# DMA landing times given to a kernel's own instruction planner, and a solve whose blocks are staged elsewhere: hybrid DeltaNet and windowed attention layer on Trainium2

## The chip, the cores and the metric

The kernel runs on one core of one Trainium2 chip. The metric is the device time of one execution in microseconds (us). Three runs of the kernel before gave 1277.84, 1278.94 and 1281.57 us; the median is 1278.94 us. Within the core, PE does matmuls and transposes, DVE, ACT and POOL are the three engines for elementwise work, and SP issues all DMA transfers of this kernel on one in-order queue. Each engine runs its instructions in the order in which they were written to it, and waits on semaphores for what it needs.

## The reference

The reference is one encoder layer on a sequence of 2048 rows of 1024. Cut to what matters here:

```python
h = rms_norm(x, norm_w)
proj = h @ w_in                      # one projection, split into ten parts
dn = fwd + bwd                       # gated DeltaNet, 4 heads of 128, both directions
sw = windowed_gqa_with_sinks(...)    # 8 query heads, window of 128
mix = concat([rms_norm(dn) * silu(dn_z), sw * silu(sw_z)])
x = x + mix @ w_out

# the DeltaNet, for each head, direction and chunk:
m     = strict_lower((k * beta) @ k.T * decay)
t_inv = inverse(eye + m)             # unit lower triangular
u, w  = t_inv @ (v * beta), t_inv @ (k * beta * exp(g))
# then a scan over the chunks with a 128x128 state:
v_new = u_i - w_i @ state
o     = (q_i * exp(g_i)) @ state + a_i @ v_new
state = state * exp(g_last) + k_dec.T @ v_new
```

The kernel works in chunks of 128 rows, so there are 16 chunks for each head and direction, and 32 triangular 128x128 matrices to be inverted for each head.

## The kernel before

**Stages.** `phase_a` normalises x, makes the projections (each product in three float32r matmuls from high and low parts, L191 to L193 and L202 to L204), the convolution, and the windowed attention. Results go to DRAM: `kq_d` and `v_d` hold keys, queries and values of the DeltaNet, `zdn_d` its gates, `mix_sw` the attention output. `phase_b` holds the DeltaNet and the output projection. Its four heads run through these steps:

- `pre_front(h)` loads keys and queries (`kq`, a ring of two buffers, L654), values (`vt`, L656) and decay rows (`dc`, L664, broadcast over the partitions), transposes them on PE, makes the Gram products `gh` on PE, scales them into `ma` on DVE (L703), and writes the triangular matrices to DRAM as `m_d` (L708).
- `solve(h)` reads back only the 32x32 diagonal blocks of the 32 matrices, four per matrix, one block to a partition. The forward direction's blocks land in the upper half of the tile `X` (L731), the other direction's in the lower half of `L` (L732). DVE copies the first, transposed, into `L` (L734). POOL then sets `X` to zero (L735) and its diagonal to one (L736), and 31 pairs of DVE instructions do the elimination (L741, L745). `X` goes to DRAM as `x_d` (L746).
- `invert(h)` brings the inverses of the blocks back, one matrix row to a partition (`xc`, L757), transposes them on DVE (`xt`, L758), and places them on the diagonals of three 128x128 work matrices `e1`, `e2`, `e3` (L763, L765, L767; all three are buffers named `iv` in the trace). Each takes four POOL copies of 32 partitions. Five batches of products `pi` (L772) then assemble the inverse in place in `ma`. This is done four times for each head, `hi` = 0 to 3.
- `scan(h)` is the serial chain over the 16 chunks, both directions interleaved: it loads `kqc` (L810), and each step goes through `pk`, `r`, `py`, `yk`, `po` and the new state `S` (L812 to L837). `post` normalises the output, applies the gate `zt` and writes `mix_dn` (L882).

The program issues scan(h), pre_front(h+1), solve(h+1), invert(h+1) for h = 0 to 2, then scan(3). Beside them, 32 units of the output projection for the attention half ("fill", products `pcs`, L599 to L601) can run at any time; each loads `mxs`, `xrs` and in the later half `zcs` into small rings. At the end `out_dn` reads `mix_dn` back as `mxd` and does the DeltaNet half (`pcd`, L561 to L563).

**The order of the work** does not follow the program text. `set_order` takes all instructions, builds their dependences (data, ring buffers, pool memory), and plans: a list scheduler runs backward and forward twelve times with an estimated duration for each instruction, keeps the forward plan with the smallest estimated end among the last five, and ties every engine's instructions to that order. A DMA is a step on SP of 500 ns; what depends on it may start after a lag of 2400 ns (`LAG["SP"]`), plus `move`, the time that its pieces take on the transfer engines by the planner's formula (`count / piece * (8 + 0.148 * piece) / 16`, in ns and elements), plus `late`, 2000 ns for a source that is broadcast over partitions. All transfers share one `bus`: a transfer starts when those planned before it have moved. Names in the planner are the tile's name, an underscore and a running number; the fixed list of first loads shows the form:

```python
first_loads = ['xr0_0_', 'nwb_', 'ident_', 'ws_kv0_0_', ...]
```

Of the kernel before, what the change touches and what calls it, by code (L numbers as in the profile page):

```python
# [7 lines left out]
F32 = mybir.dt.float32  # L8
F32R = mybir.dt.float32r
AF = mybir.ActivationFunctionType  # L10
# [5 lines left out]
P = 128  # L16
# [503 lines left out]
def phase_b(ctx, wide, late, tc, t, ident, consts, hp, mix_dn, mix_sw, kq_d, v_d, zdn_d, zsw_d, dp, out):  # L520
    nc = tc.nc
    V, A, G, T = nc.vector, nc.scalar, nc.gpsimd, nc.tensor
    dma = nc.sync.dma_start
# [93 lines left out]
    q1 = pool("q1", stack=pre_stack)  # L617
# [6 lines left out]
    quads = [slice(32 * p, 32 * p + 32) for p in range(4)]  # L624
# [100 lines left out]
    def solve(h, H):  # L725
        m_d, x_d, _ = H["solve"]
        L = qa.tile([P, 32, 32], F32, tag="L", name=f"L{h}")
        X = qa.tile([P, 32, 32], F32, tag="X", name=f"X{h}")
        lv = [m_d[d].rearrange("u (p y) -> (u p) y", p=4)[:, : 32 * P] for d in range(2)]
        lv = [a.rearrange("q (r x) -> q r x", x=P)[:, :, :32] for a in lv]  # L730
        dma(X[0:64], lv[0])  # L731
        dma(L[64:128], lv[1])  # L732
        x = X.rearrange("p r c -> p (r c)")
        V.tensor_copy(L[0:64], X[0:64].rearrange("p r c -> p c r"))  # L734
        G.memset(x, 0.0)  # L735
        G.memset(x[:, ::33], 1.0)  # L736
        for c in range(31):
            n = 31 - c
            tm = qa.tile([P, 256], F32, tag="tm", name=f"tm{h}_{c}")
            tv = tm[:, : n * (c + 1)].rearrange("p (r k) -> p r k", k=c + 1)  # L740
            V.tensor_tensor(  # L741
                tv, L[:, c + 1 :, c : c + 1].to_broadcast([P, n, c + 1]),
                X[:, c : c + 1, 0 : c + 1].to_broadcast([P, n, c + 1]), ALU.mult,
            )
            V.tensor_tensor(X[:, c + 1 :, 0 : c + 1], X[:, c + 1 :, 0 : c + 1], tv, ALU.subtract)  # L745
        dma(x_d.rearrange("d u (p r) c -> (d u p) (r c)", p=4), X.rearrange("p r c -> p (r c)"))  # L746

    def invert(h, H):
        _, x_d, mp = H["solve"]
        for hi in range(4):  # L750
            e1, p2, e2, e3 = (z[hi % len(z)] for z in zts)
            m = mp[hi]
            x0, x1 = {}, {}
            for d, c4 in ((0, hi), (1, 3 - hi)):
                xc = qb.tile([P, 4, 32], F32, tag="xc", name=f"xc{h}_{d}_{c4}", bufs=4)
                xt = qb.tile([P, 4, 32], F32, tag="xt", name=f"xt{h}_{d}_{c4}", bufs=4)
                dma(xc, x_d[d, 4 * c4 : 4 * c4 + 4].rearrange("u i c -> i u c"))  # L757
                V.transpose(xt.rearrange("p u c -> p (u c)"), xc.rearrange("p u c -> p (u c)"))  # L758
                x0[d], x1[d] = (xc, xt) if d == 0 else (xt, xc)
            g = qb.tile([P, 4, P], F32, tag="g", name=f"g{h}_{hi}", bufs=2)  # L760
            G.tensor_tensor(g, m[:, :, 0], m[:, :, 1], ALU.add)
            for p, q in enumerate(quads):
                G.tensor_copy(e1[q, :, q], x0[p % 2][q])  # L763
            for p, q in enumerate(quads):
                G.tensor_copy(e2[q, :, q], x1[1 - p % 2][q])  # L765
            for p, q in enumerate(quads):
                G.tensor_copy(e3[q, :, q], x0[p // 2][q])  # L767

            def prod(j, lhs, rhs):
                o = ps_i[(hi + j) % 2].tile([P, 4, P], F32, tag="inv", name=f"pi{j}_{h}_{hi}")  # L770
                for c in range(4):
                    T.matmul(o[:, c], lhs(c), rhs(c), start=True, stop=True)  # L772
                return o

            def half(c):
                a = m[:, c].rearrange("p s i -> p (s i)")[:, :384].rearrange("p (e x) -> p e x", x=192)
                return a[:, :, :64]

            o = prod(0, lambda c: g[:, c], lambda c: e1[:, c])
            b1 = qb.tile([P, 4, P], F32, tag="b1", name=f"b1{h}_{hi}", bufs=2)  # L780
            A.activation(b1, o, AF.Copy, scale=-1.0)
            for d in range(2):
                for q in quads:
                    G.tensor_copy(m[q, :, 1 - d, q], x1[d][q])
            o = prod(1, lambda c: e2[:, c], lambda c: b1[:, c])
            for q, r in ((1, 0), (2, 3)):
                A.activation(e3[quads[q], :, quads[r]], o[quads[q], :, quads[r]], AF.Copy)
            o = prod(2, lambda c: b1[:, c], lambda c: e2[:, c])
            for r, q in ((0, 1), (1, 0), (2, 3), (3, 2)):
                A.activation(m[quads[r], :, 1 - r % 2, quads[q]], o[quads[r], :, quads[q]], AF.Copy)  # L790
            o = prod(3, lambda c: g[:, c], lambda c: e3[:, c])
            for d in range(2):
                A.activation(p2[halves[1 - d], :, halves[d]], o[halves[1 - d], :, halves[d]], AF.Copy, scale=-1.0)
            o = prod(4, lambda c: p2[:, c], half)
            for d in range(2):
                A.activation(m[halves[d], :, 1 - d, halves[1 - d]], o[halves[d], :, halves[1 - d]], AF.Copy)
# [131 lines left out]


ENGINES = ("PE", "DVE", "Activation", "Pool", "SP")  # L930
LAG = {"PE": 205, "DVE": 140, "Activation": 160, "Pool": 120, "SP": 2400}
SAME = {"PE": 0, "DVE": 115, "Activation": 130, "Pool": 120, None: 0}

# [4 lines left out]
def set_order(tc):  # L938


    insts, boundaries = [], []
# [9 lines left out]
    def aps(l):  # L951
        return [a.bass_ap for a in l if hasattr(a, "bass_ap")]
# [47 lines left out]
    for k, (i, eng) in enumerate(insts):  # L1000
        touched = [(a, False) for a in aps(i.ins)] + [(a, True) for a in aps(i.outs)]
        for a, w in touched:
            name = a.tensor.name
# [4 lines left out]
            b = box(a, list(x.shape))  # L1008
# [17 lines left out]
    for text in boundaries:  # L1026
        op, name = text.split("op=")[1].split(" ")[0], text.split("pool=")[1].split()[0]
        p = pools[name]
# [93 lines left out]
    for k in range(total):  # L1122
        if eng[k] == "SP":
            a = aps(insts[k][0].outs)[0]
            count = a.ap[0][1] * size(a)
            piece = min(run(x) for x in aps(insts[k][0].ins) + [a])
            move[k] = count / piece * (8 + 0.148 * piece) / 16
            spread = [x.ap[0][0] == 0 for x in aps(insts[k][0].ins)]
            late[k] = 2000 * any(spread)
        lag = LAG[eng[k]] + move[k] + late[k] if k < n else 0  # L1130
        if eng[k] == "PE" and not insts[k][0].is_transpose and "float32r" not in str(insts[k][0].ins[0].dtype):
            lag += 40
        if eng[k] == "Activation" and len(aps(insts[k][0].outs)) > 1:
            lag += 90
        for s in succ[k]:
            if eng[s] == eng[k] != "SP":
                nxt[k].append((s, SAME[eng[k]] * ((k, s) in wrote)))
            else:
                nxt[k].append((s, lag))
        for s in started[k] if k < n else ():  # L1140
            nxt[k].append((s, None))
        for s, d in nxt[k]:
            prv[s].append((k, d))
# [165 lines left out]
```

## Time and profile before

| | |
|---|---|
| median of 3 runs | 1278.94 us (1277.84 to 1281.57) |
| profiled execution | 1274.25 us |
| its span (first to last instruction) | 1272.5 us |
| instructions | 22253 |
| PE busy | 1219.4 us, 96% of the span |
| DVE, ACT, POOL busy | 889.5, 703.2, 507.4 us |
| moved by DMA | 205.34 MB, mean 161 GB/s |

The page of the profile gives busy time by engine, the span in 40 equal slices of 31.8 us (busy share in tenths, and the clock granted to PE), the chain of work that ended last, and groups of instructions. Other views of the same trace answer for a stretch of time: a table of busy time by stretch, a list of who waited for whom, the instructions in order of time, and the instructions that touch one tile. "Busy" PE is an upper bound of its work, because matmuls are pipelined and their ends are modelled. A bracket behind a row of the timeline is the idle time of that engine just before the row, with what ended it.

### The profile page before, as it was taken

What the parts mean: (1) busy time and instruction counts of PE and PEld (TensorE: products, weight loads), DVE (VectorE), ACT (ScalarE), POOL (GpSimd) and SP (SyncE); (2) the same over time, 40 slices, a digit from 0 to 9 for tenths busy, and PEclk for the clock granted to TensorE, in tenths of its full rate; (3) what the DMA queues carried; (4) which work ended last, traced back from release to release, by engine and by line L of the source; (5) the groups of instructions that cost most, each with busy time, mean ns of one, the idle gap of its engine ahead of it and who ended that gap; (6) DMA issues with size and microseconds to landing.
All of it is one profiled execution on the core that took longest, in us unless ns stands there. A gap on an engine that the chain in (4) does not pass through costs nothing.

```text
span 1272.5 us, 22253 instructions
## 1 busy us (share of the span) xinstructions
PE 1219.4 (96%) x7066; PEld 1044.4 (82%) x7066; DVE 889.5 (70%) x2154; ACT 703.2 (55%) x2105; POOL 507.4 (40%) x893
## 2 busy tenths in 40 slices
PE   6999999999999999999999998998799899999998
PEld 6998877788889998787788787887688789798876
DVE  4422387999975589999986573788488879557333
ACT  6321254776644677776654425858557955566210
POOL 1330044666613398665221306613672651641000
PEclk9999999999999999999999998999899999999999
DMA  8442254322544434522137826967965974746675
GB/s 269 145 132 76 95 180 128 97 97 81 180 132 144 130 96 116 158 87 67 58 117 244 224 96 189 276 189 207 270 169 154 269 191 138 217 145 214 227 242 205
DMA packets 225510, 205.34 MB, mean 161 GB/s; under 512 B 48497, under 2 KB 175089, under 8 KB 225393
## 3 DMA queue, kind: packets, MB, share of 16 engines
q1 hardware_dynamic: 225392, 203.92, 52.7%
q8 instruction: 56, 0.92, 0.3%
q14 instruction: 62, 0.50, 0.1%
HBM read 138.79 MB, written 65.08 MB: 160 GB/s over the span
## 4 chain that ended last, share of the span: by engine, by line
PE 67%; DVE 12%; DMA 9%; ACT 7%; issue 3%; POOL 1%; SPq 0%; DVEq 0%; ACTq 0%; POOLq 0%
PE pf_c L191 4%; PE pf_c L192 4%; PE pf_c L193 4%; PE pf_z L191 4%; PE pf_z L192 4%; PE pf_z L193 4%; PE pi L772 4%; DVE acc L242 3%; PE pt L363 3%; PE pq_q L202 2%; PE pq_q L204 2%; PE pq_q L203 2%; PE pcd L561 2%; PE pcd L563 2%; PE pcd L562 2%
## 5 line engine op out<-in xcount | busy, mean ns | idle before, releaser
L191 PE MATMUL pf_c<-xhi,wh_c 128*128 128x512 f32 x384 | 151.0, 404 | 0.7 <-DVE acc L242 0.4
L192 PE MATMUL pf_c<-xlo,wh_c 128*128 128x512 f32 x384 | 150.6, 401 | 0.0
L193 PE MATMUL pf_c<-xhi,wl_c 128*128 128x512 f32 x384 | 149.1, 401 | 0.0
L242 DVE SCALAR_TENSOR_TENSOR acc<-pf_c,cw,acc 128x512 f32<-128x512 f32 (+1 forms) x192 | 140.3, 743 | 11.3 <-ACT acc L238 9.2
L358 POOL TENSOR_SCALAR pr<-pr,st 128x384 f32<-128x384 f32 (+1 forms) x128 | 80.1, 648 | 71.3 <-DVE st L356 60.0
L191 PE MATMUL pf_z<-xhi,wh_z 128*128 128x512 f32 x256 | 86.6, 401 | 0.5 <-DVE zo L215 0.5
L349 ACT ACTIVATE pr<-pr,st 128x384 f32<-128x384 f32 (+1 forms) x128 | 76.1, 596 | 19.6 <-DVE st L345 19.1
L192 PE MATMUL pf_z<-xlo,wh_z 128*128 128x512 f32 x256 | 86.2, 399 | 0.0
L191 PEld LDWEIGHTS pf_c<-xhi,wh_c 128*128 128x128 f32 x384 | 72.1, 188 | 15.3 <-DVE acc L242 1.7
L193 PE MATMUL pf_z<-xhi,wl_z 128*128 128x512 f32 x256 | 84.7, 397 | 0.0
L192 PEld LDWEIGHTS pf_c<-xlo,wh_c 128*128 128x128 f32 x384 | 72.3, 188 | 13.0
L193 PEld LDWEIGHTS pf_c<-xhi,wl_c 128*128 128x128 f32 x384 | 71.8, 188 | 13.0
L345 DVE CUSTOM_DVE_ANT_0 pr<-s,mask,sink 128x384 f32<-128x384 f32 (+1 forms) x128 | 72.5, 593 | 12.4 <-PE s L344 8.3
L367 ACT ACTIVATE ph<-pt 128x512 fp32r<-128x512 f32 x92 | 53.0, 596 | 40.9 <-PE pt L363 39.1
L826 ACT ACTIVATE yk<-py,ck 128x128 f32<-128x128 f32 x120 | 43.9, 366 | 49.5 <-PE py L821 48.4
L363 PE MATMUL pt<-ident,pr 128*128 128x128 f32 x368 | 67.2, 274 | 1.9 <-DVE q L327 1.1
L368 DVE TENSOR_TENSOR pl<-pt,ph 128x512 fp32r<-128x512 f32 x92 | 61.6, 681 | 5.1 <-ACT ph L367 5.0
L703 DVE SCALAR_TENSOR_TENSOR ma<-gh,bp,dc 128x256 f32<-128x256 f32 x128 | 54.9, 476 | 10.4 <-PE gh L694 8.7
L363 PEld LDWEIGHTS pt<-ident,pr 128*128 128x128 f32 x368 | 46.5, 140 | 17.7 <-DVE pl L368 3.0
L202 PE MATMUL pq_q<-wh_q,xhi 128*128 128x256 f32 x256 | 60.3, 285 | 0.6 <-ACT sgkv L261 0.3
L599 PE MATMUL pcs<-wohs,mhs 128*128 128x512 f32 x128 | 57.7, 451 | 2.9 <-ACT mhs L593 2.3
L814 DVE SCALAR_TENSOR_TENSOR r<-pk,negc,vs 128x128 f32<-128x128 f32 x120 | 41.5, 346 | 27.1 <-PE pk L812 26.6
(251 smaller groups left out, 3709.8 us busy)
## 6 DMA issues: line engine op xcount, KB each, us to landing
kqc<-kq_d SPq DMA_DIRECT2D x120, 128.0 KB, 3.0
ws_c<-wt SPq DMA_DIRECT2D x48, 256.0 KB, 3.3
xr<-x SPq DMA_DIRECT2D x16, 512.0 KB, 6.3
ws_z<-wt SPq DMA_DIRECT2D x32, 256.0 KB, 3.9
kq<-kq_d SPq DMA_DIRECT2D x16, 512.0 KB, 5.3
m_d<-ma SPq DMA_DIRECT2D x32, 256.0 KB, 5.4
mxs<-mix_sw SPq DMA_DIRECT2D x32, 256.0 KB, 3.8
xrs<-x SPq DMA_DIRECT2D x32, 256.0 KB, 3.6
```

Of the source, the lines that this page charges most:

```text
L191: T.matmul(ps, hi[:, k, cs], xhi[b][:, k], start=(k == 0), stop=False)
L192: T.matmul(ps, hi[:, k, cs], xlo[b][:, k], start=False, stop=False)
L193: T.matmul(ps, lo[:, k, cs], xhi[b][:, k], start=False, stop=(k == KC - 1))
L202: T.matmul(ps[:, :n], xh, hi[:, k, :n], start=(k == 0), stop=False)
L242: V.scalar_tensor_tensor(av, ps[:, lo:], cw[:, i, k : k + 1], av, ALU.mult, ALU.add)
L345: V.tensor_tensor_reduce(pr[j][:, :n], ps[:, :n], mask[:, lo * P : hi * P], 1.0, sink[:, hh : hh + 1], ALU.add, ALU.min, accum_out=nm[:, j ...
L349: A.activation(pr[j][:, :n], pr[j][:, :n], AF.Exp, bias=nm[:, j : j + 1], scale=-1.0, accum_out=den[:, j : j + 1])
L358: G.tensor_scalar(pr[j][:, :n], pr[j][:, :n], den[:, j : j + 1], 1.0, ALU.mult, ALU.mult)
L363: T.transpose(pt[:, j], pr[j][:, (kb - lo) * P : (kb - lo + 1) * P], ident)
L368: V.tensor_tensor(pl, ptf, ph.bitcast(F32), ALU.subtract)
L599: T.matmul(ps, mh[:, k], wh[:, k], start=(k == 0), stop=False)
L703: V.scalar_tensor_tensor(ma[d, c4][:, c], gh[:, k], bp[:, d, cc : cc + 1], gms[d][:, c : c + 1].to_broadcast([P, 2, P]), ALU.mult, ALU.mult,)
```

## The change

Two things are changed.

In the kernel: the forward direction's blocks of `solve` land in `lt`, a tile of the ring of two that holds `kq`, instead of in `X`. So the two memsets of `X` need nothing of this head's load and stand ahead of the copy into `L`, which reads `lt`. In `invert`, for `hi` = 0 only, the four copies into `e1` go to DVE, those into `e2` stay on POOL, and those into `e3` go to ACT; for `hi` = 1 to 3 all stay on POOL.

In the planner: a table `LANDS` gives, for names that begin with one of 21 strings and go on with a digit, the time from issue to landing in ns. Where it is longer than 2400 + `move` + `late`, `late` is raised so that the lag equals it. Every engine's order is planned anew with these lags.

```diff
@@ solve
         X = qa.tile([P, 32, 32], F32, tag="X", name=f"X{h}")
...
-        dma(X[0:64], lv[0])
+        lt = q1.tile([P, 2, 512], F32, tag="kq", name=f"lt{h}", bufs=2).rearrange("p a s -> p (a s)")
+        lt = lt.rearrange("p (r c) -> p r c", c=32)
+        dma(lt[0:64], lv[0])
         dma(L[64:128], lv[1])
         x = X.rearrange("p r c -> p (r c)")
-        V.tensor_copy(L[0:64], X[0:64].rearrange("p r c -> p c r"))
         G.memset(x, 0.0)
         G.memset(x[:, ::33], 1.0)
+        V.tensor_copy(L[0:64], lt[0:64].rearrange("p r c -> p c r"))
@@ invert
-            for p, q in enumerate(quads):
-                G.tensor_copy(e1[q, :, q], x0[p % 2][q])
-            for p, q in enumerate(quads):
-                G.tensor_copy(e2[q, :, q], x1[1 - p % 2][q])
-            for p, q in enumerate(quads):
-                G.tensor_copy(e3[q, :, q], x0[p // 2][q])
+            for s, a, b in zip("GGG" if hi else "VGA", (e1, e2, e3), ([0, 1, 0, 1], [1, 0, 1, 0], [0, 0, 1, 1])):
+                xs = x1 if a is e2 else x0
+                for q, k in zip(quads, b):
+                    if s == "A":
+                        A.activation(a[q, :, q], xs[k][q], AF.Copy)
+                    else:
+                        (V if s == "V" else G).tensor_copy(a[q, :, q], xs[k][q])
@@ planner
+LANDS = {"m_d": 5400, "x_d": 5500, "xc": 3300, "X": 4600, "L": 4600, "lt": 4600, "kq": 5300, "vt": 5100, "dc": 6100, "zt": 5100, "mix_dn": 3900, "mxd": 4000, "xrd": 4900, "mxs": 3800, "xrs": 3600, "zcs": 3900, "kqc": 3000, "xr": 6000, "xt": 6200, "woss": 4600, "wosd": 4600}
 LAG = {"PE": 205, "DVE": 140, "Activation": 160, "Pool": 120, "SP": 2400}
@@ set_order
             late[k] = 2000 * any(spread)
+            base = aps(insts[k][0].outs)[0].tensor.name
+            for form, lands in LANDS.items():
+                if base.startswith(form) and base[len(form)].isdigit():
+                    late[k] = max(late[k], 1.0 * (lands - LAG["SP"] - move[k]))
```

## The prediction

> **What bounds the kernel now.** I read the page first: busy time, the slices and the granted clock.
>
> ```profile
> span 1272.5 us, 22253 instructions
> ...
> PE 1219.4 (96%) x7066; PEld 1044.4 (82%) x7066; DVE 889.5 (70%) x2154; ACT 703.2 (55%) x2105; POOL 507.4 (40%) x893
> ...
> PEclk9999999999999999999999998999899999999999
> ```
>
> PE is the bound, and all that a new order can take away is its idle time, 1272.5 - 1219.4 = 53.1 us, and the half-clock time behind it: the two eights, in slices 24 and 28 (763 to 795 and 891 to 922 us). The table by stretch says where the idle time lies (columns: stretch, its length, busy us of PE, PEld, DVE, ACT, POOL, the clock, the DMA engines' share, GB/s).
>
> ```profile
> 0.00:770.00 770.00, 752.11 (x4102) 636.58 (x4103) 558.73 (x1212) 414.25 (x1022) 318.19 (x505) 1.00 0.42 131
> 770.00:930.00 160.00, 141.04 (x899) 123.46 (x898) 107.41 (x315) 110.18 (x439) 76.53 (x150) 0.95 0.80 231
> 930.00:980.00 50.00, 48.28 (x350) 44.21 (x349) 44.80 (x131) 33.04 (x117) 27.54 (x51) 1.00 0.51 154
> 980.00:1030.00 50.00, 44.95 (x299) 38.78 (x297) 39.82 (x125) 40.42 (x176) 30.75 (x70) 1.00 0.87 244
> 1030.00:1160.00 130.00, 126.94 (x935) 116.21 (x935) 91.37 (x281) 78.33 (x276) 49.91 (x116) 1.00 0.58 169
> 1160.00:1272.50 112.50, 106.10 (x491) 85.13 (x489) 47.37 (x95) 27.02 (x81) 4.53 (x3) 1.00 0.68 229
> ```
>
> PE idles 17.9 us in the first 770, 19.0 from 770 to 930, 1.7, 5.1, 3.1 and 6.4 us in the others. The two loose stretches are those in which one head's scan ends while the next head is prepared, and the DMA engines are 80 to 87% busy there. The list of PE's waits from 770 to 1030 names what came late:
>
> ```profile
> PE tr L674 <- DMA kq<-kq_d: 4.7, 3, 3.9
> PE gh L694 <- DVE ma L703: 3.7, 3, 2.4
> PE pk L812 <- DVE S L837: 2.9, 1, 2.9
> ```
>
> Columns: total us, times, longest. Finer stretches show what the longest of them cost besides:
>
> ```profile
> 786.00:793.00 7.00, 3.14 (x18) 2.98 (x17) 2.56 (x6) 4.46 (x15) 4.26 (x14) 0.67 1.00 281
> 898.00:903.00 5.00, 2.15 (x7) 0.98 (x5) 3.22 (x11) 2.69 (x17) 2.19 (x2) 0.81 1.00 319
> 903.00:908.00 5.00, 5.00 (x14) 3.79 (x15) 2.52 (x6) 3.10 (x11) 1.81 (x5) 0.51 0.89 231
> ```
>
> Around the wait of 3.9 us the clock is 0.67 of full; after the 2.85 idle us of 898 to 903 it is 0.51, so the next 5 us of work hold 2.5 us of loss.
>
> **The landing times.** The list of DMA issues has the times that the table repeats (columns: count, KB, median us to landing):
>
> ```profile
> kqc<-kq_d SPq DMA_DIRECT2D x120, 128.0 KB, 3.0
> ...
> kq<-kq_d SPq DMA_DIRECT2D x16, 512.0 KB, 5.3
> m_d<-ma SPq DMA_DIRECT2D x32, 256.0 KB, 5.4
> ...
> xrs<-x SPq DMA_DIRECT2D x32, 256.0 KB, 3.6
> ...
> x_d<-X SPq DMA_DIRECT2D x4, 512.0 KB, 5.5
> xc<-x_d SPq DMA_DIRECT2D x32, 64.0 KB, 3.3
> ```
>
> By the planner's formula the lags were 2.83 us for kqc (256 pieces of 128 elements: 2.4 + 0.43), 3.74 for kq, 3.26 for m_d, 3.07 for xrs, 3.68 for x_d, 2.81 for xc. So kqc, the commonest, moves by 0.17 us; kq by 1.56; and the round trip m_d, lt, x_d, xc by 2.14 + 0.57 + 1.82 + 0.49 = 5.0 us for each head. No instruction is added or dropped by this part. What it can do is put other work ahead of a consumer that is held, and a load ahead in SP's queue. One case of each stands in the timeline: SP, then DVE.
>
> ```profile
> 917.58 4.91 SPq L589 DMA_DIRECT2D zcs<-zsw_d  x1
> 922.53 0.61 SPq L732 DMA_DIRECT2D L<-m_d  x1
> ```
>
> ```profile
> 922.78 0.69 DVE L602 TENSOR_TENSOR xrs<-xrs,pcs 128x512 f32<-128x512 f32 x1 [4.22 <-DMA xrs<-x]
> 923.39 0.28 DVE L837 COPY S<-po 128x128 f32<-128x128 f32 x1
> ```
>
> DVE stood 4.22 us before a fill's addition, with the first state of scan(1) queued behind it; that is PE's wait of 2.9 us. SP's issue of zcs held everything behind it for 4.9 us.
>
> The price of this part cannot be read from a row. Its bounds: best, half of the 24.1 us idle in the two loose stretches and the two losses at half clock come back, 12 + 2.3 + 2.5 = 16.8; worst, it adds holds (below). I take half of the two waits that a late transfer caused, (4.7 + 2.9) / 2 = 3.8 us, nearest to the rows that name a DMA, and the clock of the first episode, 0.33 x 7 = 2.3 us, since the kq wait is the longest. Together 6.1. The wait for ma (3.7) is DVE's own load; it stays.
>
> The Trainium skill, page TensorE: Matmul & The Clock Gate, section on the HAM clock gate, says that PE's clock is halved after an idle window of about 3.4 us and released after as long a busy one. The 0.67 beside a 3.9 us wait agrees; the 0.51 after idle pieces of which the longest is 2.4 does not need a gap that long. By the page halving the kq wait surely returns the 2.3; by the rows a remaining 2 us might not, and the sum would be 2.3 smaller.
>
> **The solve.** Its start in head 1, DVE and then POOL:
>
> ```profile
> 831.97 1.08 DVE L734 COPY L<-X 64x1024 f32<-64x1024 f32 x1
> 833.86 0.35 DVE L833 SCALAR_TENSOR_TENSOR S<-S,egt,po 128x128 f32<-128x128 f32 x1 [0.81 <-PE po L830]
> 834.54 0.69 DVE L594 TENSOR_TENSOR mls<-mxs,mhs 128x512 fp32r<-128x512 f32 x1 [0.34 <-ACT mhs L593]
> ...
> 836.49 0.21 DVE L741 TENSOR_TENSOR tm<-L,X 128x31 f32<-128x31 f32 x1
> ```
>
> ```profile
> 833.11 0.95 POOL L735 MEMSET X<- 128x1024 f32 x1 [6.88 <-DVE L L734]
> ...
> 835.33 0.15 POOL L736 MEMSET X<- 128x32 f32 x1
> ```
>
> The elimination starts 836.49 - 833.05 = 3.4 us after the copy, and the memsets (0.95 + 0.15) stand in that gap. After the change they are done before, on a POOL that sat idle 6.88 us. But DVE idled only 0.81 + 0.34 = 1.15 us of the gap: the rest was work that must be done anyway. So 0 to 3.4 us for each of the heads 1 to 3; I take 1.0 for the first, nearer to the idle time, and 0.5 for the second together with the third: 1.5 on the path. The copy itself stays, and the transfers keep size and count. The spare kq buffer costs nothing as long as the copy is over before pre_front(h+1) wants its second kq. Head 2's first keys came to PE here, 20 us after head 1's copy:
>
> ```profile
> 853.85 0.60 PE L674 MATMUL tr<-ident,kq 128*128 128x128 f32 x4
> ```
>
> **The diagonal copies.**
>
> ```profile
> L763 POOL COPY iv<-xc x32: 279/286/709, 767.1 to 1116.9; 32x128 f32<-32x128 f32 x32
> ...
> L787 ACT ACTIVATE iv<-pi x32: 268/268/271, 778.6 to 1153.3; 32x128 f32<-32x128 f32 x32
> ```
>
> Columns: min/median/max ns. Eight of POOL's twelve copies leave it for hi = 0: 8 x 0.286 = 2.3 us. ACT gains 4 x 0.268 = 1.1 us, in a stretch where it is busy 110 of 160. DVE gains four; nearest is its 128x128 COPY above at 0.28, so at most 1.1 us. In head 1 the first group began at 906.8 and its first product came soon after:
>
> ```profile
> 906.76 0.61 POOL L763 COPY iv<-xc 32x128 f32<-32x128 f32 x2 [3.07 <-DMA xc<-x_d]
> ...
> 908.75 0.62 POOL L765 COPY iv<-xt 32x128 f32<-32x128 f32 x2
> ```
>
> ```profile
> 906.74 0.60 DVE L758 STREAM_TRANSPOSE xt<-xc 128x128 f32<-128x128 f32 x2 [1.65 <-DMA xc<-x_d]
> ```
>
> POOL finished e1 and e2 together at 909.4. DVE is free of its transposes at 907.3, and four copies end at 908.5 at the latest; POOL's four for e2 end at about the same time. So 0.9 us for the start, up to 2.3 where the copies into ma (behind e3 on POOL) are awaited. Bounds 0 to 2.3 per head, against them 1.1 on DVE; I take 0.5 for heads 1 and 2 each: 1.0.
>
> The Trainium skill, GPSIMD Engine Reference, Specifications, says that POOL's SBUF port is shared with DVE where DVE copies with both ports. POOL's 709 ns maximum agrees that it can be slowed. By the page e2 would take up to 4 x 0.709 = 2.8 us beside DVE's copies, and the term would be below zero by about 1.
>
> **The sum.** 6.1 + 1.5 + 1.0 = 8.6 us back. Against it, all engines are ordered anew, the full stretches too: the 17.9 idle us of the first 770 are mostly the opening, and I charge a tenth of it, 1.8. Net 6.8: span 1265.7, the execution 1.75 more (1274.25 - 1272.5), 1267.4. The profiled execution was 4.69 below the median of the runs, so 1272 for the median.
>
> **The rivals.**
>
> - *No change.* In both gaps the DMA share is 1.00 (786 to 793, 898 to 903): kq came late because the engines were full, and no order on SP makes 281 to 319 GB/s more. The planner counted the bus already, and a measured landing has the queue in it, so waiting is counted twice. Besides, the table misses some of what it names: the planner's names are tile, underscore, number, so `mix_dn_` and `wosd_` are not followed by a digit and stay as they were, and `X` is no longer loaded. Only 18 of 21 entries act, and the tail's write and re-read keep their lags. Then the 6.1 is 0, and 2.5 - 1.8 = 0.7 is left: 1278.
> - *Slower: SP is held in the scans.* With loads believed to take 1.5 to 2 us longer, the plan puts more of them ahead of the kqc of the scan, each waiting on SP for a ring buffer, as zcs did for 4.91 us. In 930 to 980 and 1030 to 1160 PE is full (1.7 and 3.1 us idle), so a hold there costs its 4.9 and a piece at half clock, 2.5: 7.4 us. One hold eats the gain; it decides from the second. Two: 1272 + 14.8 = 1287. For it: SP is in order, rings are of two, the loose stretches have no room left on the DMA engines. Against it: kqc runs in a ring of four, and the plan models buffers.
> - *Much faster.* The gaps at 786 and 898 close: the best bound, 16.8, gives 1262.
>
> **How the numbers follow.** Forecast (faster by about 7) 0.40, much faster 0.08, no change 0.17, slower 0.35. A measurement tells about 0.3% from nothing here: 3.8 us, 1275.1 to 1282.8. So faster 0.48, same 0.17, slower 0.35. The forecast's own range is 1266 to 1275; 8 in 10 needs both signs: from 1262 to 1290, two holds and a little, leaving out a third hold (1294).
>
> **What would show it.** L735 before L734 in every head, and the first tm within 1 us of the copy when DVE is free. In 770 to 930, PE busy above 141 with less time for the same products, the wait tr <- kq below 4.7 in total, no S behind an addition that waits for xrs, a clock above 0.95. The first 770 us within 2 us of now. Wrong would be: PE idle growing in 930 to 980 or 1030 to 1160 with kqc as releaser and SP waiting before it; or pre_front's loads held by lt.

## The result, and the profile after

The changed kernel takes 1287.82 us (median of 4 runs, 1286.57 to 1290.91) beside 1279.33 us for the kernel before (4 runs, 1277.84 to 1281.57). The ratio is 1.0074, 95% interval 1.0057 to 1.0091: slower by some 8.5 us, where 6.9 us faster was forecast. The profiled execution took 1286.57 us, 12.3 more than the one of before. But that one lies 5.1 us below the median of its kernel, the one of after 1.3 below; so of the differences read from the two traces some 4 us are the spread between executions.

The page of the profile after:

```profile
span 1284.8 us, 22219 instructions
...
PE 1226.8 (95%) x7066; PEld 1047.2 (82%) x7066; DVE 892.1 (69%) x2170; ACT 707.6 (55%) x2121; POOL 507.1 (39%) x861
...
PEclk9999999999999999999999996999999999999999
```

PE has the same 7066 matmuls but is busy 7.4 us longer, and idles 58.0 us where it was 53.1. The 6 in the clock row is slice 24, counted from 0 as in the prediction (771 to 803 us). The table by stretch, with the columns as in the prediction:

```profile
0.00:770.00 770.00, 749.64 (x4089) 633.14 (x4090) 548.01 (x1186) 414.79 (x1026) 322.09 (x497) 1.00 0.42 130
770.00:930.00 160.00, 139.64 (x839) 118.91 (x838) 114.63 (x341) 105.36 (x421) 71.17 (x134) 0.91 0.75 214
930.00:980.00 50.00, 47.88 (x359) 44.59 (x358) 39.61 (x107) 33.50 (x111) 29.63 (x56) 1.00 0.66 191
980.00:1030.00 50.00, 43.97 (x264) 35.88 (x263) 43.33 (x145) 40.27 (x184) 20.07 (x29) 0.97 0.78 229
1030.00:1160.00 130.00, 127.76 (x943) 118.04 (x941) 91.76 (x276) 79.43 (x274) 58.33 (x143) 1.00 0.59 171
```

The two full stretches, 930 to 980 and 1030 to 1160, are as full as before (2.1 and 2.2 us idle, before 1.7 and 3.1). Most of the loss is in the stretch from 770 to 930, where PE gets through 839 matmuls instead of 899. The waits of PE from 770 to 1030 (total us, times, longest):

```profile
PE trv L711 <- ACT jk L682: 4.6, 4, 2.0
PE gh L694 <- DVE ma L703: 3.3, 4, 1.0
PE tro L881 <- ACT oacc L878: 2.7, 4, 1.1
PE tr L674 <- DMA kq<-kq_d: 1.8, 1, 1.8
```

The wait for `kq` fell from 4.7 to 1.8 us, and of the waits for a state `S` (2.9 us) 0.2 is left: what the table was to remove, it mostly removed. Waits for ACT have grown instead: that of the value transposes `trv` from 2.4 to 4.6 us, because all transposes of keys and values go through one output buffer, which ACT has to read before the next group, and that of `tro` from 2.0 to 2.7.

**Where the time went.** The `pk` product of a scan step marks how far the scans are. Its group between 885 and 907 us ends with the last step of scan(0), first in the kernel before, then after (the last number before the forms is the start of the last one):

```profile
L812 PE MATMUL pk<-S,kqc x6: 275/275/275, 885.8 to 889.9; 128*128 128x128 f32 x6
```

```profile
L815 PE MATMUL pk<-S,kqc x15: 275/275/294, 884.8 to 904.2; 128*128 128x128 f32 x15
```

Scan(0) ends 14.3 us later. PE has begun 4826 of its matmuls by then in the kernel before and 4823 in the changed one, so this is a loss and not work that was moved. From there to the end of the span it is 1284.8 - 904.2 = 380.6 us, beside 1272.5 - 889.9 = 382.6. So the whole loss is made before scan(0) ends, and the three later heads together are 2.0 us shorter. A slower execution of the order of before (e8 below, where only some copies change their engine) ends scan(0) at 893.9 us; so the traces say 10 to 14 us, not more exactly.

In the timeline the first `tm` of head 0's solve stands at 750.5 us (before 728.6). One reason can be read from the transposes of head 0's keys and values. Their last three groups start at 700.6, 703.3 and 705.6 us before; the last:

```profile
705.59 0.60 PE L674 MATMUL tr<-ident,kq 128*128 128x128 f32 x4
```

After, they start at 713.7, 718.3 and 721.3:

```profile
721.32 0.60 PE L674 MATMUL tr<-ident,kq 128*128 128x128 f32 x4
```

They were put 13 to 16 us further back among the last projections. These projections (`pf_z`) give PE work while the solve runs. Before, they end at 774.4 us, and the first product `pi` of the inverse follows 0.3 us behind them:

```profile
774.71 1.06 PE L772 MATMUL pi<-iv,g 128*128 128x128 f32 x8
```

After, they end at 778.0, and the first `pi` comes 22.3 us behind them:

```profile
777.11 0.86 PE L193 MATMUL pf_z<-xhi,wl_z 128*128 128x512 f32 x3
...
800.27 2.04 PE L775 MATMUL pi<-iv,g 128*128 128x128 f32 x8 [1.63 <-POOL iv L770]
```

In between PE has only head 1's preparation, in pieces, and its clock is halved:

```profile
777.00:782.00 5.00, 2.99 (x18) 2.18 (x17) 2.86 (x8) 4.24 (x20) 0.90 (x1) 1.00 0.65 223
782.00:806.00 24.00, 17.59 (x63) 13.86 (x63) 14.06 (x39) 15.02 (x62) 11.28 (x22) 0.51 0.99 269
806.00:811.00 5.00, 4.54 (x31) 3.96 (x30) 2.84 (x7) 4.27 (x17) 3.34 (x11) 0.97 0.84 251
```

17.59 busy us at a clock of 0.51 are 9.0 us at full speed: with 6.4 idle and 8.6 lost to the clock, 15.0 of the 24 us are gone. Before, too, these stretches are not full: the 24 us behind the last projection (774.4 to 798.4) hold 19.59 busy us at a clock of 0.86, or 16.8 at full speed. So about 8 of the 15 are new.

What SP did between the write of `x_d` and the loads of `xc` that wait for it, before and then after:

```profile
760.71 0.32 SPq L746 DMA_DIRECT2D x_d<-X  x1
765.12 6.30 SPq L757 DMA_DIRECT2D xc<-x_d  x5
```

```profile
777.94 0.54 SPq L748 DMA_DIRECT2D x_d<-X  x1
778.89 0.32 SPq L218 DMA_DIRECT2D zdn<-zo  x1
...
783.14 0.54 SPq L656 DMA_DIRECT2D vt<-v_d  x1
783.73 2.26 SPq L813 DMA_DIRECT2D kqc<-kq_d  x3
786.03 0.60 SPq L759 DMA_DIRECT2D xc<-x_d  x1
```

Before, SP issued nothing between them: the write landed 4.39 us behind its issue, and the load went out at once. After, eleven other transfers were planned into the believed 5.5 us. The write landed sooner, after 3.43 us, but the load went out 8.1 us behind it, 4.7 us later than it could have.

**The edits of solve and invert** did what they say. Head 1 on DVE (POOL's memset of `X` had started at 782.1 us):

```profile
842.16 1.07 DVE L738 COPY L<-lt 64x1024 f32<-64x1024 f32 x1
...
843.87 0.20 DVE L743 TENSOR_TENSOR tm<-L,X 128x31 f32<-128x31 f32 x1
```

The elimination starts 0.64 us behind the copy's end, where it was 3.4. In heads 2 and 3 it is 0.4 and 0.3 us (before 3.1 and 2.5).

### The profile page after: what moved, and what is told of

Same layout as the page of the kernel before. It is cut to its first block, busy times and chain, and to the rows that moved or that the text cites. A ratio compares the mean times of both kernels' runs of the same rounds, so it can differ in the third digit from the quotient of the medians.

```text
span 1284.8 us, 22219 instructions
## 1 busy us (share of the span) xinstructions
PE 1226.8 (95%) x7066; PEld 1047.2 (82%) x7066; DVE 892.1 (69%) x2170; ACT 707.6 (55%) x2121; POOL 507.1 (39%) x861
## 4 chain that ended last, share of the span: by engine, by line
PE 70%; DVE 9%; ACT 7%; DMA 7%; issue 3%; POOL 3%; SPq 0%; DVEq 0%; ACTq 0%; POOLq 0%
PE pf_c L191 5%; PE pf_c L192 5%; PE pf_c L193 5%; PE pi L775 4%; PE pf_z L192 4%; PE pf_z L191 4%; PE pf_z L193 4%; PE pt L363 3%; PE pcd L562 2%; PE pcd L561 2%; PE pcd L563 2%; PE pcs L599 2%; PE pcs L600 2%; PE po L833 2%; PE py L824 2%
## 5 line engine op out<-in xcount | busy, mean ns | idle before, releaser
L242 DVE SCALAR_TENSOR_TENSOR acc<-pf_c,cw,acc 128x512 f32<-128x512 f32 (+1 forms) x192 | 139.9, 743 | 16.6 <-ACT acc L238 13.5
L358 POOL TENSOR_SCALAR pr<-pr,st 128x384 f32<-128x384 f32 (+1 forms) x128 | 83.2, 669 | 88.2 <-DVE st L356 71.6
L367 ACT ACTIVATE ph<-pt 128x512 fp32r<-128x512 f32 x92 | 53.1, 594 | 39.8 <-PE pt L363 33.6
L703 DVE SCALAR_TENSOR_TENSOR ma<-gh,bp,dc 128x256 f32<-128x256 f32 x128 | 55.0, 477 | 19.4 <-PE gh L694 17.5
L684 POOL TENSOR_TENSOR nk<-ssk,pw 128x4 f32<-128x4 f32 x16 | 16.6, 1035 | 114.5 <-DVE ssk L683 114.4
L203 PE MATMUL pq_q<-wh_q,xlo 128*128 128x256 f32 x256 | 60.3, 283 | 0.0
```

Of the source, the lines that this page charges most:

```text
L203: T.matmul(ps[:, :n], xl, hi[:, k, :n], start=False, stop=False)
L242: V.scalar_tensor_tensor(av, ps[:, lo:], cw[:, i, k : k + 1], av, ALU.mult, ALU.add)
L358: G.tensor_scalar(pr[j][:, :n], pr[j][:, :n], den[:, j : j + 1], 1.0, ALU.mult, ALU.mult)
L703: V.scalar_tensor_tensor(ma[d, c4][:, c], gh[:, k], bp[:, d, cc : cc + 1], gms[d][:, c : c + 1].to_broadcast([P, 2, P]), ALU.mult, ALU.mult,)
```

## The experiments

All kernels below compute the whole layer; they differ in the two edits, the table, and the planner. Three theories were tested first. A: head 0's preparation and solve are planned too late, because the longer lags re-order them. B: the spare `kq` buffer of the edits costs the next head its keys. C: the landing times count waiting twice, wherever they stand. The kernel before ran beside every group of experiments, with a median of 1277.6 to 1278.9 us; each ratio below is to those runs.

### The two halves of the change

`e1_edits_only` leaves out the table and the lines that use it, `e2_landings_only` the two edits:

```diff
-            base = aps(insts[k][0].outs)[0].tensor.name
-            for form, lands in LANDS.items():
-                if base.startswith(form) and base[len(form)].isdigit():
-                    late[k] = max(late[k], 1.0 * (lands - LAG["SP"] - move[k]))
```

> The edits of solve and invert with the old lags. Theory A (the longer lags made the planner put head 0's preparation late, solve(0) started 22 us later, 750 against 728, and PE ran dry at 778 at half clock): the solve starts by 735 and the time is 1272 to 1281, no slower than before. Theory B (the spare key buffer does it: lt holds the ring of kq until 749, head 1's keys load at 749 instead of 704): this kernel has all of the loss, 1286 to 1290.

> The table of landing times with the old solve and invert. Theory A: all of the loss or more, 1285 to 1291, first tm of head 0 past 745. Theory B: nothing of it, 1276 to 1282.

Measured: the edits alone 1283.08 us, ratio 1.0028 (1.0014 to 1.0042); the table alone 1294.49 us, 1.0120 (1.0105 to 1.0135). Each loses. Theory A fails as it was stated: without any longer lag, e1 has its first `tm` at 750.0 us all the same. B fails too, since its 1286 to 1290 was not reached. e2 is slower than either theory allowed. In both, scan(0) ends at 902.5 us, nearly as late as with both changes; the row of e1:

```profile
L815 PE MATMUL pk<-S,kqc x14: 275/275/377, 885.1 to 902.5; 128*128 128x128 f32 x14
```

From there to the end e1 needs 378.6 us, 4.0 less than before, and e2 389.5, 6.9 more. So the edits gain behind scan(0) and the table loses there, and a new plan of either kind ends scan(0) 12 to 14 us later than the trace of before. In e1 that is mostly phase A: its projections end at 786.2 us instead of 774.4, and the first `pi` follows 2.0 us behind them. The stretch of the first 640 us, before and then e1:

```profile
0.00:640.00 640.00, 622.85 (x3502) 531.32 (x3503) 469.39 (x1005) 359.86 (x856) 295.43 (x469) 1.00 0.40 124
```

```profile
0.00:640.00 640.00, 614.80 (x3446) 525.86 (x3447) 462.25 (x978) 353.68 (x838) 294.57 (x465) 0.99 0.38 122
```

56 matmuls fewer at 622.85 / 3502 = 0.178 us are 10.0 us. The same row of the changed kernel has 3485, or 3.0 us: there the larger part is lost behind 770 us.

### Head 0 first

`e3_head0_first` is the changed kernel with 10 us of urgency (in the forward plan they count as due 10 us sooner) for the instructions that write the tiles of head 0's preparation and solve; `e4_before_head0_first` is the kernel before with the same lines.

```diff
+    first = [10000 * any(re.match("kq0_|tr0_|ssk0_|nk0_|bp0_|gh0_|ma0_|dc0_|jk0_|ks0_|m_d0_|L0_|lt0_|X0_|tm0_|x_d0_|trv0_|vs0_|vt0_|ssq0_", a.tensor.name) for a in aps(i.outs)) for i, _ in insts]
-        now = plan([-(b + d) for b, d in zip(back[1], dur)], True)
+        now = plan([-(b + d) - f for b, d, f in zip(back[1], dur, first)], True)
```

> The changed kernel, and in the forward pass of the planner every instruction that writes a tile of head 0's preparation or solve counts as 10 us more urgent. Theory A: solve(0) starts before 735, no long stretch at half clock near 780, and 10 to 13 of the 12 us lost by the end of head 0 come back: 1272 to 1279. Theory C (longer lags are counted twice and spread waits everywhere, the late solve is a symptom): the solve starts early but the time stays at 1284 or above.

> Control: the kernel before with the same urgency for head 0. Its solve(0) was in time already, so theory A expects no gain, 1277 to 1284. If it is faster by more than 0.4%, the urgency is a gain of its own and the run before this one says less on the cause.

Measured: e3 1276.12 us, ratio 0.9984 (0.9962 to 1.0006); e4 1281.04 us, 1.0022 (1.0002 to 1.0042). The first `tm` of e3 is at 734.2 us, and scan(0) ends early again:

```profile
L815 PE MATMUL pk<-S,kqc x8: 272/275/377, 886.2 to 892.1; 128*128 128x128 f32 x8
```

Urgency for one head gives back the whole loss of the change, and gives the kernel before nothing (it is 0.2% slower). `lt` still takes a `kq` buffer here, so B falls as the cause of the loss. It did hold keys back: in the changed kernel head 1's first load of `kq` was issued at 749.4 us, right behind the copy, where it was 703.9. But in e5 below, the second fastest kernel here, it comes later still, at 759.5.

### The first 640 us kept

The next kernels hold every instruction that the plan of before began within its first 640 us in that plan's order on its engine (`EARLY`, a table of those times); only the rest is planned anew. `xr` and `xt`, which load in that part alone, are out of the table in all of them.

```diff
+    early = np.frombuffer(zlib.decompress(base64.b85decode(EARLY)), np.int32).tolist()
+    fixed = {k: t for k, t in enumerate(early) if t > 0}
+    for e in ENGINES:
+        row = sorted((t, k) for k, t in fixed.items() if eng[k] == e)
+        for (_, a), (_, b) in zip(row, row[1:]):
+            nxt[a].append((b, None))
+            prv[b].append((a, None))
```

Nothing else changed (e10), the edits (e5), the table (e9), both (e6), and both with e3's urgency (e7):

> Nothing changed but that the first 640 us are kept in the order of the kernel before, so that the rest is planned anew under the same condition as in e5. Theory (the edits gain the 7 us of e5): 1276 to 1281, as the kernel before. Rival (the gain is that of a second plan, not of the edits): 1269 to 1273.

> The two edits of solve and invert without the table, and every instruction that the kernel before's plan began in its first 640 us kept in that plan's order on its engine; only what comes behind is planned anew. If the 4 us that the edits alone lost came from the new order of phase A (theory): at equal PE work within 2 us of the kernel before up to 640 us, and 1272 to 1277 for the whole. If the edits themselves cost it (rival): 1281 to 1285 again, the loss coming behind 750 us.

> The table alone (solve and invert as before; xr and xt left out), with the first 640 us kept in the order of the kernel before. With the edits, e6 took 6 us more than e5. If the table costs that much by itself (theory): 1280 to 1287, first tm of head 0 at 742 us or later. If the table harms only through phase A (rival): 1275 to 1280.

> The changed kernel with the first 640 us kept in the order of the kernel before; xr and xt, which only those transfers use, are left out of the table. Theory (head 0's preparation is planned late by the longer lags): the first tm of head 0 still comes at 742 to 752 us, its clock is lost behind it, and the time is 1281 to 1288. Rival (the whole loss comes from the new order of phase A): the time is 1274 to 1279 with the first tm near 730.

> As e6_kept_after, with head 0's preparation and solve given 10 us of urgency in the forward plan. Theory: first tm of head 0 at 728 to 740 us, at most 7 us at half clock between 760 and 830 us, 1269 to 1276 us. Rival (longer lags cost time behind head 0 as well): 1280 or more with the first tm early.

| | median us | ratio to before | 95% interval |
|---|---|---|---|
| e10, nothing | 1274.62 | 0.9970 | 0.9952 to 0.9987 |
| e5, edits | 1270.99 | 0.9942 | 0.9930 to 0.9955 |
| e9, table | 1287.27 | 1.0066 | 1.0042 to 1.0090 |
| e6, both | 1276.97 | 0.9993 | 0.9977 to 1.0010 |
| e7, both, head 0 first | 1273.81 | 0.9964 | 0.9951 to 0.9976 |

Three readings. The order of the first part is worth 1287.82 - 1276.97 = 10.9 us to the changed kernel, 12.1 to the edits (e1 against e5) and 7.2 to the table (e2 against e9). e6 was expected at 1281 or more, and that was a miss: its first `tm` is at 745.6 us, hardly earlier than after, and the first `pi` still comes 15.4 us behind the last projection, yet scan(0) ends at 893.8 us:

```profile
L815 PE MATMUL pk<-S,kqc x8: 272/275/377, 887.6 to 893.8; 128*128 128x128 f32 x8
```

So a late solve of head 0 is not enough for the loss; A holds only together with the rest of the first part. And the table still costs: 12.7 us without the edits, 6.0 with them, and 4.5 with head 0 first in both (e7 against e11 below, whose urgency is 5 us instead of 10). The control e10, between its two expectations, shows what a new plan gives by itself, here 4.2 us for nothing; the edits are worth 3.6 beyond it, with intervals that just overlap.

Along this path the medians add up: -4.2 us for the new plan behind the first part (e10), -3.6 for the edits (e5), +6.0 for the table (e6), +10.9 for the new order of the first part (after, which also has the rows of `xr` and `xt`), together 9.0 us over the kernel before.

### The copies on three engines

`e8_same_order_copies` keeps the whole order of before; only the copies into `e1` and `e3` for `hi` = 0 change their engine.

```diff
+            for s, a, b in zip("GGG" if hi else "VGA", (e1, e2, e3), ([0, 1, 0, 1], [1, 0, 1, 0], [0, 0, 1, 1])):
```

> All instructions of the kernel before in its own order, only that for hi = 0 the copies into e1 run on DVE and those into e3 on ACT, at the places in time where POOL had them. The prediction's step says 0 to 2.3 us for each of the heads 1 and 2 and took 1.0 in all: 1277 to 1279 for the whole, and the first products of the inverse 0.5 to 2 us earlier after their loads. Rival (the copies only take DVE's and ACT's time from the scan): 1280 to 1283.

Measured: 1278.91 us, ratio 1.0011 (0.9994 to 1.0028), no difference. The interval spans 4.3 us, so the 1.0 of the prediction could not have been seen in it. From the first `xc` issue to the first product in head 1 it took 4.8 us, before 5.2.

### Which rows of the table

`e12_kept_no_fill_rows` is e6 without `mxs`, `xrs`, `zcs`, `woss`. The others are e5 with a part of the table: the loads of the preparation (e13), the round trip through DRAM (e14), the rest (e15). `e17_table_no_round_trip` is e9 without the round trip's rows.

```diff
+LANDS = {"m_d": 5400, "x_d": 5500, "xc": 3300, "X": 4600, "L": 4600, "lt": 4600}
```

> e6 without the table's four rows of the fills (mxs, xrs, zcs, woss). If these put fills and their loads ahead of head 0's preparation: first tm at 728 to 738 us and 1270 to 1275. If it is the rows of the preparation itself (kq, vt, dc, m_d): first tm at 742 to 750 and 1276 to 1281, as in e6.

> The edits, phase A kept, and of the table only the rows of the preparation's loads (kq, vt, dc). Without a table (e5) 1270.99, with all rows (e6) 1276.97. If these loads' lags are what costs: 1275 to 1279, with PE's waits of the value transposes for ACT above those of e5 (1.6 us). If not: 1269 to 1274.

> As e13, with the rows of the round trip through DRAM alone (m_d, lt, L, x_d, xc), 5 us longer for each head by the planner's formula. If the plan gives those 5 us away by beginning each head's solve and inverse later than the chip needs: 1275 to 1280, with head 3's solve ending at 1075 us or later (e5: 1070.5). If not: 1269 to 1274.

> As e13, with the remaining rows alone (kqc, zt, the fills, the tail). e12, without the fill rows, was no faster than e6, so these rows should cost little: 1269 to 1274. If the scan's or the fills' rows cost: 1275 to 1279.

> e9 (table alone, phase A kept, 1287.27 us; without the table 1274.62) without the rows of the round trip (m_d, L, X, x_d, xc). If these rows carry the loss: 1272 to 1279, with the two handovers from scan 0 to 1 and 1 to 2 (last pk of one to first pk of the next) back from 38 to 24 to 34 us each. If the other rows lose as much without the edits: 1282 to 1288.

| | median us | ratio to before | 95% interval |
|---|---|---|---|
| e12, without fill rows | 1279.86 | 1.0016 | 0.9998 to 1.0034 |
| e13, `kq`, `vt`, `dc` | 1272.77 | 0.9962 | 0.9945 to 0.9978 |
| e14, `m_d`, `lt`, `L`, `x_d`, `xc` | 1286.52 | 1.0062 | 1.0037 to 1.0088 |
| e15, the rest | 1273.74 | 0.9966 | 0.9950 to 0.9982 |
| e17, table alone without round trip | 1276.73 | 0.9990 | 0.9977 to 1.0003 |

Against e5's 1270.99 the round trip's rows cost 15.5 us alone, beyond the 4 to 9 expected if they cost at all; the two other groups cost 1.8 and 2.8, which is not told apart from nothing. Taken out of e9 they return 10.5 of 12.7. The fills' rows are not the cause: without them e12 is no faster than e6. (e15 has the latest solve of all, first `tm` at 752.4 us, and its first `pi` comes 28.2 us behind the last projection. Its scan(0) ends at 898.3 us, 4.6 later than in e5, and its rest is 2.8 shorter: again the late head 0 alone does not decide.) What happens is what the `x_d` rows above show. SP around head 3's last write of `m_d` in e14, and then in e5:

```profile
1038.40 0.39 SPq L708 DMA_DIRECT2D m_d<-ma  x1
1039.54 0.32 SPq L603 DMA_DIRECT2D part<-xrs  x1
1040.80 0.32 SPq L586 DMA_DIRECT2D mxs<-mix_sw  x1
1041.17 0.43 SPq L759 DMA_DIRECT2D xc<-x_d  x1
1041.65 0.50 SPq L885 DMA_DIRECT2D mix_dn<-zt  x1
1043.93 0.52 SPq L813 DMA_DIRECT2D kqc<-kq_d  x1
1044.56 0.55 SPq L596 DMA_DIRECT2D xrs<-x  x1
1045.98 0.59 SPq L813 DMA_DIRECT2D kqc<-kq_d  x1
1046.61 0.61 SPq L733 DMA_DIRECT2D lt<-m_d  x1
```

```profile
1019.23 0.45 SPq L708 DMA_DIRECT2D m_d<-ma  x1
1021.42 0.32 SPq L603 DMA_DIRECT2D part<-xrs  x1
1021.84 0.38 SPq L883 DMA_DIRECT2D zt<-zdn  x1
1022.31 1.97 SPq L586 DMA_DIRECT2D mxs<-mix_sw  x1
1024.37 0.38 SPq L885 DMA_DIRECT2D mix_dn<-zt  x1
1024.85 0.61 SPq L733 DMA_DIRECT2D lt<-m_d  x1
```

The load of `lt` goes out 8.2 us behind the write instead of 5.6, behind seven transfers instead of four. Yet this write landed equally fast in both, 3.45 us behind its issue in e14 and 3.42 in e5 (the median of all 32 writes of `m_d` is 5.1 us in both). The load could have gone out then; it went out 4.8 us later in e14, 2.2 in e5. It is the same with `x_d`: over heads 1 to 3 the first load of `xc` goes out, in the mean, 2.5 us behind the landing of the write in e14. In the other kernels with the round trip's rows that is 1.3 to 4.2 us, in those without them 0.1 to 1.4.

From the timelines, as a mean over heads 1 to 3: the way from the end of the last Gram product to the start of the copy into `L`, and from the issue of the write of `x_d` to the first `pi`; then the two handovers (end of a scan's last `pk` to the start of the next scan's first), and the time from the last `pk` of scan(0) to the end.

| | to the copy | to `pi` | handovers 0-1, 1-2 | rest |
|---|---|---|---|---|
| before | 19.8 | 13.0 | 33.5, 23.0 | 382.6 |
| after | 22.1 | 14.7 | 29.8, 31.4 | 380.6 |
| e5, edits | 17.3 | 13.0 | 26.4, 24.0 | 375.8 |
| e10, nothing | 19.0 | 13.0 | 32.8, 25.3 | 380.0 |
| e6, both | 21.1 | 16.5 | 32.3, 27.4 | 379.1 |
| e14, round trip rows | 22.3 | 17.5 | 39.8, 31.7 | 393.8 |
| e9, table alone | 24.3 | 16.1 | 37.9, 37.6 | 393.5 |
| e17, e9 without round trip | 16.6 | 12.6 | 28.9, 31.7 | 379.3 |
| e15, the rest | 17.0 | 17.0 | 22.5, 26.1 | 373.0 |

The 5.0 us that the table adds to a head's round trip in the plan became 5.0 + 4.5 = 9.5 us on the chip (e14 against e5), and the handovers grew by 13.4 and 7.7 us. That the rows make the way longer is shown. How much of it reaches the end is another matter: e6 has the same rows and a way nearly as long, but its handovers grew by 5.9 and 3.4 us and its rest by 3.3 us alone, and e15 has a long second half and the shortest rest. The rest goes with the two handovers: their sum is 48.6 to 61.2 us where it is 373.0 to 382.6, and 71.5 and 75.5 where it is 393.8 and 393.5. Why e14 hands over so much later than e6 is not shown.

### The size of the lag

`e16_double_table` doubles what each row adds to the formula (e6 is the single one); `e18_short_round_trip` is e5 with the round trip's lags 1 us shorter instead.

```diff
-                    late[k] = max(late[k], 1.0 * (lands - LAG["SP"] - move[k]))
+                    late[k] = max(late[k], 2.0 * (lands - LAG["SP"] - move[k]) - late[k])
```

```diff
-                    late[k] = max(late[k], 1.0 * (lands - LAG["SP"] - move[k]))
+                    late[k] -= 1000
```

> As e6 (whole table, edits, phase A kept), with each row's excess over the formula doubled. If longer lags cost time by themselves: more than e6's 1276.97, 1282 to 1292, and solves that end later. If e6's loss is only the chance of another plan: 1270 to 1279.

> e5 (edits alone, phase A kept, 1270.99 us), with the planner's lags of m_d, lt, L, x_d and xc shortened by 1 us each instead of lengthened. If a longer lag costs because other transfers are planned into it ahead of the next step of the round trip: fewer of them stand between the last m_d write and the load of lt, the loads are issued at most 5.5 us behind it, and the time is 1264 to 1271. If a lag below the landing only makes SP wait with the others behind it: 1272 to 1280.

Measured: e16 1296.74 us, ratio 1.0145 (1.0116 to 1.0175); e18 1276.86 us, 0.9991 (0.9975 to 1.0007). None, one and two times the table give 1270.99, 1276.97 and 1296.74 us: it grows with the lag. Shorter lags do not turn its sign, though, and the theory behind e18 missed. The way to the copy falls to 15.3 us, but that from `x_d` to `pi` is 15.2 instead of 13.0, and nothing is won; the 5.9 us that e18 loses are not much more than the spread between plans (4.2 in e10). Of the sizes tried, that of the formula was the best.

### The best version

`e11_kept_edits_first` is e5 with 5 us of urgency for head 0.

> e5 (edits alone, phase A kept) with 5 us of urgency for head 0's preparation and solve. In e5 the first tm came at 740.5 us. Theory (a late solve of head 0 costs what the projections beside it no longer cover): first tm at 728 to 735, 1266 to 1271. Rival (at 740 it is still covered): 1270 to 1274.

Measured: 1269.32 us, ratio 0.9936 (0.9913 to 0.9960). It is not told apart from e5 (0.9930 to 0.9955), and though its first `tm` comes at 729.9 us, scan(0) ends at 896.6, no earlier than e5's 893.7. Both beat the kernel before by 7 to 10 us, and both are the edits without the table.

## Why the prediction was wrong

- **The table, 6.1 us back: wrong in sign.** Its first step held: the `kq` wait went from 4.7 to 1.8 us, more than the half taken, and most of the `S` wait left. The 2.3 us for the clock did not come: PE stood at half clock when that wait ended, at 793.2 us. In the kernel before, the clock fell at 788.4 us, 1.9 us into the wait of 3.9 (786.5 to 790.4); half of that wait was enough there. What the working missed stood in its own list, the round trip m_d, lt, x_d, xc "in all 5.0 us for each head", to which no price was given. Its rows cost 15.5 us alone (e14). Under like conditions the whole table costs 6.0 us (e6 against e5) to 12.7 (e9 against e10). C stands in part: a lag longer than the landing is filled with other transfers on SP, and the next step of the round trip stands behind them. And one figure stood for all writes: the four of `x_d` landed after 4.39, 6.56, 6.72 and 3.23 us in the kernel before, and the table has 5.5.
- **The re-ordering, 1.8 us charged: mis-sized, and the step that decided.** It should have stood at about 11 by the medians, 10 to 14 by the traces: scan(0) ends that much later. e3 and e6 take this away by two ways and return 11.7 and 10.9 us. The charge was a tenth of the idle time of the first 770 us. But a new order can add to what is lost there: in the changed kernel the projections end 3.5 us later and then leave 22.3 us, mostly at half clock, ahead of the first `pi`; in e1 they end 11.8 us later. That was not weighed.
- **The solve and the copies, 2.5 us: about right.** The gap closed to 0.3 to 0.6 us in heads 1 to 3, in head 1 with the memsets done 60 us earlier. The edits are worth 3.6 us in e5 against e10, whose intervals just overlap. The copies' share, 1.0, was too small to be seen (e8).
- **The slower rival** named the time, 1287, but by luck, for it had another place. No hold is seen in 930 to 980 and 1030 to 1160. SP's order did matter, in the handovers and for the round trip, not by ring buffers in the scans.
- **The rival of no change** had the right objection, that a landing measured in the profile already holds the queue. It took this to be worth nothing; it costs.
- **What would show it.** Memsets ahead, first `tm` within 1 us in heads 1 to 3, the lower `kq` wait and no `S` behind an addition came as said. PE busy above 141 and the clock above 0.95 in 770 to 930 did not (139.64 and 0.91), and the first 770 us hold 2.5 us less work of PE, not within 2. Of the signs of being wrong one came: `lt` held loads of pre_front, head 1's until 749.4 us; e5 shows that this need not cost.

**Open.** Why a plan made anew ends scan(0) some 10 us later when either half of the change is in it (e1, e2, after), while that of e4 loses 7.4 by its trace (897.3 against 889.9), is not settled. That the order of the first part does most of it is shown (e5 and e6, less so e9); which instructions make it is not, and a late head 0 is no common cause, since e6 and e15 have it without such a loss. Nor do the parts add: table and edits together (e6) are 6.7 us better than the sum of their own effects on e10 would give (1274.62 + 12.65 - 3.63 = 1283.64). A spread of some 3 to 4 us between plans, as e10 and e4 show it, lies on every single comparison here.

## What to carry to other kernels

A landing time read from a trace belongs to the order in which it was measured, and a median hides how far single transfers lie apart. Put into this planner as a lag, it was filled with other transfers, and the chain through memory got longer by more than the lag (9.5 us for 5.0). Try such a table by groups of rows, and look first at the transfers that follow one another. Where a change re-plans a whole program, hold the part that it does not concern in its old order, and measure the new plan without the change beside it; otherwise the scatter between plans is taken for the change's worth.

## What was not expected of the hardware

The half clock lasted long, and it began without a long gap. In the changed kernel the longest wait ahead of it is 2.0 us. PE was busy 73% of the 24 us from 782 to 806 and stayed at about half. Two finer rows of the table by stretch (the clock is the third number from the end):

```profile
798.00:802.00 4.00, 2.37 (x12) 2.00 (x11) 3.77 (x9) 2.58 (x8) 3.70 (x9) 0.50 1.06 286
802.00:806.00 4.00, 4.00 (x17) 3.64 (x17) 3.15 (x9) 2.89 (x9) 1.67 (x3) 0.50 1.01 282
```

Cut finer still, the traces show that the clock changed only at steps of 3.41 us. From 780 us on these are 788.43, 795.26, 901.07, 907.90, 924.97 and 928.38 us in the kernel before (2, 31, 2, 5 and 1 steps apart); 782.44 and 806.34 in the changed one are 7 steps apart. It rose behind a step in which PE was busy throughout; behind one with 2.95 us busy (901.07 to 904.49, before) it stayed at half. The three steps ahead of a fall in the kernel before had PE busy for 1.03 to 1.49 us, the one ahead of 782.44 for 1.40.

By the Trainium skill, page TensorE: Matmul & The Clock Gate, part on the HAM clock gate, full speed returns behind a sustained busy stretch of about 3.4 us, and the clock falls behind an idle window of about as long. For the return, the steps here agree. For the fall they differ, since none of these four steps was idle throughout; the measurement decides.

Two executions of one order can differ as much as the change: the profiled one of e8, which has the order of before but for the engine of some copies, took 1282.80 us, that of before 1274.25, while their medians, run beside each other, are 1278.91 and 1278.35. Differences of that size between two profiles say where to look; only the medians say how much.
